# Two heads of an output pair worked together in two attentions, their value products alternating between the column halves of TensorE

## The chip, the cores and the metric

The kernel runs on one core of a Trainium2 chip. The metric is device time in microseconds (us). Three runs of the kernel before took 1254.60, 1258.07 and 1257.58 us; their median is 1257.58 us. The trace used below is one profiled execution, whose span from the first to the last instruction is 1254.4 us.

## The reference, cut to what matters

Two layers of a first block and then one layer of a second block are computed for 256 tokens of 1024 features. All of it is float32. Each layer multiplies the tokens by wide matrices, and beside that works several small attentions. Two of these are touched here.

The first block's sparse attention has 8 heads of 64 features in 2 groups. For 256 tokens its selected and its window part reduce to two causal attentions over the same 256 tokens, with different keys and values:

```
s_s = einsum('bgrqd,bgqnld->bgrqnl', qb, k_g);  p_s = masked_softmax(s_s, mask_s)
o_s = einsum('bgrqnl,bgqnld->bgrqd', p_s, v_g)
p_w = masked_softmax(einsum('bgrqd,bgkd->bgrqk', qb, kwb), mask_w)
o_w = einsum('bgrqk,bgkd->bgrqd', p_w, vwb)
return gb[..., 0:1] * o_c + gb[..., 1:2] * o_s + gb[..., 2:3] * o_w
```

The second block's block attention has 8 heads of 64 features. With 256 tokens there is one block, so it is one causal attention with a slope per head:

```
lo = where(dist_o >= 0, einsum('bhqd,bhkd->bhqk', qc, ko) * scale - slopes * dist_o, -inf)
out = einsum('bhqk,bhkd->bhqd', softmax(lo), vo)
```

Each head's result, transposed, has 64 rows. Two heads lie above each other in one tile of 128 rows: an output pair.

## The kernel before

**Main work.** The wide products split each float32 operand into a high and a low part (`hi`, `lo`; `hh`, `hl` for the activations) and multiply three times on TensorE. A unit of weights is 128 x 1024: it is loaded by a DMA to `raw`, copied by ScalarE to `hi` (line 435) and subtracted by VectorE to `lo` (line 439). Each sixth high part is made by GpSimd instead (line 433). While the convolution of the second block runs on VectorE, each fourth low part is made by GpSimd instead (line 437). There are four buffers for `hi` and four for `lo`.

**Order.** TensorE's instructions stand in the order in which Python emits them; a scheduler orders the other engines. The small attentions are generators. `mm` and `tr` add an estimated TensorE time to a clock; `yield 5100.0` in a generator means "go on when that clock is 5.1 us further", and `pump`, called inside the wide products, lets the generators that are due emit their next step. So a `yield` between two steps stands for the time the other engines have for what lies between them. TensorE itself never changes the order: a matmul that waits stops all behind it.

**PSUM.** Score and transpose tiles (`psm`) share three banks in turn; the results of attentions (`pso`) have one.

**Sparse attention of the first block** (`nsa_att`, run once in each of two layers). Head `2*pr + j` belongs to output pair `pr` (0 to 3) and lies in the rows `64*j` to `64*j + 63`. `scores0(pp, j)` works the first 128 queries of the heads of two pairs with one `j`, `scores1(pr, j)` the last 128 queries of one head; each with both branches (`w`), maximum (lines 895, 916), exponential (899, 920), sum, gate and scaling (905, 925). `transp(pr, j)` transposes one head's probabilities of both branches and copies them to `pts` (938 on ScalarE, 940 on VectorE). `pv(pr, j)` multiplies them with the values; output rows are the half `j`, so all four products of a call use one half of TensorE's columns. The scores of a head are emitted one head ahead of its transposes.

**Block attention of the second block** (`moba`). `scores(pp, j)` multiplies 64 rows (half `j`) of queries and keys and adds slope times distance by a bfloat16 product of all 128 rows (`SLP`, `DM`); the two kinds alternate. Two heads of one `j` are worked, then transposed and multiplied with the values one after the other, in one half of the columns each.

**Other places that have the same form.** In `nsa_cmp` (line 782) four products with 32 output rows each, at four column positions, are emitted in turn. In `gla` (the tiles `pas`) products of 64 rows alternate between the two row halves.

**The convolution** (`conv`) of the second block is 31 taps for each of four tiles on VectorE (lines 1432, 1435), emitted two taps per 1.5 us of the clock. `moba` runs beside it.

Of the kernel before, what the change touches and what calls it, by code (L numbers as in the profile page):

```python
# [98 lines left out]
def block_kernel(ctx, tc, x_in, mem_in, positions, ln_mix, w_in, b_merge, nsa_q_norm, nsa_k_norm,  # L99
# [778 lines left out]
    def nsa_att(VV, GT, T, c_mem, oh, ol):  # L878
# [7 lines left out]
        def scores0(pp, j):  # L886
            p0 = PS()
            for a in range(2):
                o0 = p0[:, 256 * a:256 * a + 256].rearrange("p (w k) -> p w k", w=2)
                q = QS[:, 4 * pp + 2 * a + j, 0:P]  # L890
# [12 lines left out]
            dve.tensor_tensor(r02, r02, gt4[:, 0, 4 * pp + j:4 * pp + j + 3:2, 1:3], op=OP.mult)  # L903
            for c in range(4):
                dve.tensor_scalar(e0[:, c], e0[:, c], r0[:, c:c + 1], None, op0=OP.mult)
            E0[pp, j] = e0
# [21 lines left out]
        def transp(pr, j):  # L928
            e0, e1 = E0[pr // 2, j], E1.pop((pr, j))
            res = []  # L930
            for w in range(2):
                pt = PS()
                tr(pt[:, 0:P], e0[:, 2 * (pr % 2) + w], IDF)
                for kt in range(2):
                    tr(pt[:, P + kt * P:2 * P + kt * P], e1[:, w, kt * P:kt * P + P], IDF)
                pts = T2("pts")[:, 0:384]
                if w == 0:
# [16 lines left out]
        order = [(2 * pp + a, j) for pp in range(2) for j in range(2) for a in range(2)]  # L954
        scores0(0, 0)
        yield 500.0
        scores1(*order[0])
# [421 lines left out]
    def layer_2(hT):  # L1379
# [105 lines left out]
        def moba():  # L1485
            UE = {}

            def scores(pp, j):
                rr = slice(64 * j, 64 * j + 64)
                p0, p1 = PS(), PS()  # L1490
                for a in range(2):
                    pr = 2 * pp + a
                    sl = SLP[:, 2 * pr + j, :]
                    mm(p0[:, a * P:a * P + P], CQ[rr, pr, 0:P], CK_[rr, pr, 0:P], True, False)
                    mm(p0[:, a * P:a * P + P], sl, DM[:, 0:P], False, True)
                    mm(p1[:, a * 256:a * 256 + 256], CQ[rr, pr, P:256], CK_[rr, pr, :], True, False)
                    mm(p1[:, a * 256:a * 256 + 256], sl, DM[:, P:384], False, True)
                n = SM([P, 4], "n0")
                dve.tensor_reduce(n[:, 0:2], v2(p0[:, 0:256]), op=OP.max, axis=AX, negate=True)
                dve.tensor_reduce(n[:, 2:4], v2(p1), op=OP.max, axis=AX, negate=True)  # L1500
                e0 = T2("pexp", (2, 128))
                e1 = T2("pexp", (2, 256))
                s = SM([P, 4], "s0")
                for a in range(2):
                    act(e0[:, a], p0[:, a * P:a * P + P], AF.Exp, bias=n[:, a:a + 1], accum_out=s[:, a:a + 1])
                    act(e1[:, a], p1[:, a * 256:a * 256 + 256], AF.Exp, bias=n[:, 2 + a:3 + a],
                        accum_out=s[:, 2 + a:3 + a])
                r = SM([P, 4], "r0")
                dve.reciprocal(r, s)
                for a in range(2):  # L1510
                    dve.tensor_scalar(e0[:, a], e0[:, a], r[:, a:a + 1], None, op0=OP.mult)
                    dve.tensor_scalar(e1[:, a], e1[:, a], r[:, 2 + a:3 + a], None, op0=OP.mult)
                UE[pp, j] = (e0, e1)

            for pp in range(2):
                yield from take_po()
                po = PO()
                for j in range(2):
                    rr = slice(64 * j, 64 * j + 64)
                    scores(pp, j)  # L1520
                    yield 9950.0
                    e0, e1 = UE.pop((pp, j))
                    for a in range(2):
                        h = 2 * (2 * pp + a) + j
                        pt = PS()
                        tr(pt[:, 0:P], e0[:, a], IDF)
                        for kt in range(2):
# [150 lines left out]
```

## Time and profile before

| what | value |
|---|---|
| runs (us) | 1254.60, 1257.58, 1258.07; median 1257.58 |
| span of the profiled execution | 1254.4 us |
| TensorE busy | 1234.7 us, 98% |
| VectorE busy | 846.5 us, 67% |
| ScalarE busy | 596.6 us, 48% |
| GpSimd busy | 244.6 us, 19% |
| weight loads of TensorE | 1108.0 us, 88% |
| HBM | 167 GB/s over the span |

The profile gives no time for the profiled execution beside its span; the span lies 0.2 us under the fastest of the three runs. "Busy" of TensorE counts a matmul from its start to the modelled end of its results, and matmuls overlap, so what a matmul costs TensorE is read from the distance between two starts, not from its duration. A float32 product appears as two records. Rows of one line, operation and tile that follow each other are merged, with their count (x8).

### The profile page before, as it was taken

The numbers are of one execution on the slowest core, as the hardware profiler recorded it, in microseconds if no ns is written. First come the engines' busy times: TensorE is split into PE (matmuls) and PEld (weight loads), VectorE is DVE, ScalarE is ACT, GpSimd is POOL, SyncE is SP. The second block draws the span as 40 slices with busy tenths as digits, with TensorE's granted clock in tenths as the row PEclk, the third lists the DMA queues.
The fourth block names the chain that finished last, engine by engine and source line by source line (L and its number), as shares of the span: only waits on it lengthen the run. The fifth ranks groups of instructions, "written<-read, shape, count | busy, mean of one in ns | idle before, by whom it ended". The sixth has DMA issues, their size and how long they took to land.

```text
span 1254.4 us, 21138 instructions
## 1 busy us (share of the span) xinstructions
PE 1234.7 (98%) x8317; PEld 1108.0 (88%) x8317; DVE 846.5 (67%) x1356; ACT 596.6 (48%) x956; POOL 244.6 (19%) x246
## 2 busy tenths in 40 slices
PE   8999999999999999999999999999999999999997
PEld 6897799998899899888799998989998988899996
DVE  5867878566754545567978566654545899956756
ACT  6567544444644444556644434544434343453532
POOL 2300320122112112200320023121211122111213
PEclk9999999999999999999999999999999999999999
DMA  8557533466566666656623566565665654445562
GB/s 269 177 157 203 155 101 102 137 185 199 185 185 185 189 183 196 184 153 173 191 68 112 155 167 190 177 193 179 198 187 171 202 155 137 153 135 169 179 219 74
DMA packets 165559, 211.00 MB, mean 168 GB/s; under 512 B 12065, under 2 KB 132277, under 8 KB 165460
## 3 DMA queue, kind: packets, MB, share of 16 engines
q1 hardware_dynamic: 165172, 209.49, 55.9%
q8 instruction: 65, 1.06, 0.3%
q0 software_dynamic: 288, 0.16, 0.1%
q14 instruction: 34, 0.28, 0.1%
HBM read 208.74 MB, written 1.05 MB: 167 GB/s over the span
## 4 chain that ended last, share of the span: by engine, by line
PE 84%; DVE 8%; POOL 2%; ACT 2%; issue 2%; DMA 0%; SPq 0%; POOLq 0%; ACTq 0%; DVEq 0%
PE acc L188 59%; PE psm L188 18%; PE psm L192 3%; PE pso L188 3%; DVE lo L439 3%; DVE b8x L1435 2%; POOL M L1150 2%; ACT hi L435 1%; PE acc L782 1%; ACT b8x L527 1%; DVE gate L1149 0%; DVE b8x L528 0%; DVE QB L1046 0%; ACT pexp L920 0%; DMA gtmp<-in_mem_norm 0%
## 5 line engine op out<-in xcount | busy, mean ns | idle before, releaser
L439 DVE TENSOR_TENSOR lo<-raw,hi 128x1024 fp32r<-128x1024 f32 (+1 forms) x359 | 451.5, 1261 | 264.0 <-ACT hi L435 203.5
L435 ACT ACTIVATE hi<-raw 128x1024 fp32r<-128x1024 f32 (+1 forms) x314 | 330.0, 1057 | 415.4 <-PE acc L188 254.7
L188 PE MATMUL acc<-hh,hi 128*128 128x256 f32 x960 | 278.7, 290 | 0.4 <-ACT hi L435 0.4
L188 PE MATMUL acc<-hh,lo 128*128 128x256 f32 x960 | 272.0, 283 | 1.7 <-DVE lo L439 1.6
L188 PE MATMUL acc<-hl,hi 128*128 128x256 f32 x960 | 271.9, 283 | 0.0
L188 PEld LDWEIGHTS acc<-hh,hi 128*128 128x128 f32 x960 | 184.0, 192 | 4.1 <-issue 2.5
L188 PEld LDWEIGHTS acc<-hh,lo 128*128 128x128 f32 x960 | 184.0, 192 | 2.3 <-DVE lo L439 2.3
L188 PEld LDWEIGHTS acc<-hl,hi 128*128 128x128 f32 x960 | 184.1, 192 | 1.1 <-DVE hl L528 0.2
L433 POOL TENSOR_SCALAR hi<-raw 128x1024 fp32r<-128x1024 f32 x55 | 67.0, 1219 | 477.8 <-PE acc L188 319.7
L188 PE MATMUL psm<-hh,hi 128*128 128x256 f32 x448 | 126.8, 283 | 0.0
L188 PE MATMUL psm<-hh,lo 128*128 128x256 f32 x448 | 126.8, 283 | 0.0
L188 PE MATMUL psm<-hl,hi 128*128 128x256 f32 x448 | 126.8, 283 | 0.0
L188 PE MATMUL acc<-hi,b8x 128*128 128x512 f32 (+1 forms) x336 | 104.0, 384 | 0.1
L188 PE MATMUL acc<-hi,oh 128*128 128x512 f32 x256 | 100.2, 391 | 0.0
L188 PE MATMUL acc<-lo,oh 128*128 128x512 f32 x256 | 99.8, 390 | 0.0
L188 PE MATMUL acc<-hi,ol 128*128 128x512 f32 x256 | 99.6, 389 | 0.0
L188 PE MATMUL acc<-hi,hh 128*128 128x512 f32 (+1 forms) x224 | 90.0, 402 | 0.0
L188 PE MATMUL acc<-lo,hh 128*128 128x512 f32 (+1 forms) x224 | 84.8, 378 | 2.2 <-DVE lo L439 2.2
L188 PEld LDWEIGHTS psm<-hl,hi 128*128 128x128 f32 x448 | 86.0, 192 | 0.5
L188 PEld LDWEIGHTS psm<-hh,hi 128*128 128x128 f32 x448 | 86.0, 192 | 0.5
L188 PEld LDWEIGHTS psm<-hh,lo 128*128 128x128 f32 x448 | 86.0, 192 | 0.0
L188 PE MATMUL acc<-hi,hl 128*128 128x512 f32 (+1 forms) x224 | 84.8, 378 | 0.0
(369 smaller groups left out, 2151.5 us busy)
## 6 DMA issues: line engine op xcount, KB each, us to landing
raw<-in_w_in SPq DMA_DIRECT2D x160, 512.0 KB
raw<-in_w_up SPq DMA_DIRECT2D x64, 512.0 KB
raw<-in_w_down SPq DMA_DIRECT2D x64, 512.0 KB
raw<-in_w_branch SPq DMA_DIRECT2D x28, 512.0 KB
raw<-in_w_out SPq DMA_DIRECT2D x24, 512.0 KB
raw<-in_cmp_w SPq DMA_DIRECT2D x32, 256.0 KB
raw<-in_mem_w_kv SPq DMA_DIRECT2D x15, 512.0 KB
raw<-in_w_branch SPq DMA_DIRECT2D x16, 256.0 KB
```

The costliest lines, as they stand in the source:

```text
L188: nc.tensor.matmul(o, l, r, start=start, stop=stop, skip_group_check=True)
L192: nc.tensor.transpose(o, i, ident)
L433: pool.tensor_scalar(hi, raw, 1.0, 1.0, op0=OP.mult, op1=OP.mult)
L435: act(hi, raw, AF.Copy)
L439: dve.tensor_tensor(lo, raw, f32(hi), op=OP.subtract)
L527: act(hi, src, AF.Copy, scale=scale)
L782: nc.tensor.matmul(ph[32 * j:32 * j + 32, k * 256:k * 256 + 256], R[k][:, lp].rearrange("p a b -> p (a b)"), rv[:, j, :], start=q == 0, st ...
L1150: pool.tensor_tensor(fl(M), fl(M), fl(g), op=OP.add)
L1435: dve.scalar_tensor_tensor(CV[:, cb], GLU[:, cb, t:t + 256], CWT[:, cb, t:t + 1], CV[:, cb], op0=OP.mult, op1=OP.add)
```

## The change

In both attentions the unit of work becomes the output pair, with both its heads. The products with the values then go head 0, head 1, head 0, head 1, so that consecutive products use the lower and the upper half of TensorE's columns in turn.

- `nsa_att`: `scores0(pr)` takes the first 128 queries of both heads of one pair; `transp(pr, w)` and `pv(pr, w)` take one branch of both heads. Per pair the steps are: scores1 of both heads, 5.1 us, transposes of branch 0, 2.0 us, products of branch 0, transposes of branch 1, scores0 of the next pair, 2.0 us, products of branch 1. The number of products, transposes and softmax steps stays.
- `moba`: `scores(pr)` emits the four 64-row products of a pair in turn, row half 0 and 1, in two banks, and then the four bfloat16 products. Maximum, reciprocal and scaling are done head by head, so there are 16 maxima where there were 8, and 8 reciprocals where there were 4. The scores of a pair are emitted before the transposes of the pair before it. The products with the values go by pair.

The core of the diff:

```diff
-        def pv(pr, j, po, pts2):
-            rr = slice(64 * j, 64 * j + 64)
-            vs = slice(64 * j, 64 * j + 64)
+        def pv(pr, w, po, t):
             a = pr % 2
-            o = po[rr, 256 * a:256 * a + 256]
-            for w, pts in enumerate(pts2):
-                mm(o, VVv[:, 0, w, vs], pts[:, 0:256], a == 0 and w == 0, False)
-                mm(o[:, 128:256], VVv[:, 1, w, vs], pts[:, 256:384], False, False)
+            for kt in range(2):
+                for j in range(2):
+                    js = slice(64 * j, 64 * j + 64)
+                    o = po[js, 256 * a + P * kt:256 * a + 256]
+                    mm(o, VVv[:, kt, w, js], t[j][:, 256 * kt:256 + P * kt], a == 0 and w == 0 and kt == 0, False)
...
-        for n, (pr, j) in enumerate(order):
+        for pr in range(4):
             pp = pr // 2
-            if n + 1 < 8:
+            for j in range(2):
                 yield 850.0
-                if n % 2 == 1:
-                    scores0(order[n + 1][0] // 2, order[n + 1][1])
-                scores1(*order[n + 1])
+                scores1(pr, j)
             yield 5100.0
-            t = transp(pr, j)
-            yield 3350.0
-            if n % 4 == 0:
+            t = transp(pr, 0)
+            yield 2000.0
+            if pr % 2 == 0:
                 yield from take_po()
                 po = PO()
-            pv(pr, j, po, t)
-            if n % 4 == 3:
+            pv(pr, 0, po, t)
+            t = transp(pr, 1)
+            if pr + 1 < 4:
+                scores0(pr + 1)
+            yield 2000.0
+            pv(pr, 1, po, t)
...
+            def scores(pr):
+                p = [PS(), PS()]
+                for q0, k1 in ((0, P), (P, 256)):
+                    for j in range(2):
+                        rr = slice(64 * j, 64 * j + 64)
+                        mm(p[j][:, q0:q0 + k1], CQ[rr, pr, q0:q0 + P], CK_[rr, pr, 0:k1], q0 == 0, False)
                 for j in range(2):
...
+                    mm(p[j][:, 0:P], sl, DM[:, 0:P], False, True)
+                    mm(p[j][:, P:384], sl, DM[:, P:384], False, True)
...
+                if pr + 1 < 4:
+                    yield 3000.0
+                    scores(pr + 1)
+                yield 6500.0
+                t = [transp(e) for e in UE.pop(pr)]
+                yield 2000.0
...
+                for kt in range(2):
+                    for j in range(2):
+                        h = 2 * pr + j
+                        o = po[64 * j:64 * j + 64, 256 * a + P * kt:256 * a + 256]
+                        mm(o, CVv[kt][:, h * 64:h * 64 + 64], t[j][:, 256 * kt:256 + P * kt], kt == 0, kt == 1)
```

**TensorE, products with the values of the sparse attention, first layer.** Here pts_285 and pts_287 are the two transposed tiles of a `transp`. Before, they are the two branches of one head:

```order
L188 MATMUL pso_293_1556<-pts_285_1501,n2_92_550 64x256
L188 MATMUL pso_293_1556<-pts_285_1501,n2_92_550 64x128
L188 MATMUL pso_293_1556<-pts_287_1507,n2_92_550 64x256
L188 MATMUL pso_293_1556<-pts_287_1507,n2_92_550 64x128
```

Now they are the two heads of a pair in one branch:

```order
L188 MATMUL pso_290_1538<-pts_285_1501,n2_92_550 64x256
L188 MATMUL pso_290_1538<-pts_287_1507,n2_92_550 64x256
L188 MATMUL pso_290_1538<-pts_285_1501,n2_92_550 64x128
L188 MATMUL pso_290_1538<-pts_287_1507,n2_92_550 64x128
```

A call still has four products; the 256-wide and the 128-wide one of the two halves now follow each other.

**TensorE, scores of the block attention.** The products of two g4 tiles have 64 rows, those of SLP and DM are bfloat16 and have 128. Before, for the two heads of one row half:

```order
L188 MATMUL psm_1845_10861<-g4_1783_10452,g4_1782_10451 128x128
L188 LDWEIGHTS SLP_10813
L188 MATMUL psm_1845_10861<-DM_10822,SLP_10813 128x128
L188 MATMUL psm_1846_10862<-g4_1783_10452,g4_1782_10451 128x256
L188 LDWEIGHTS SLP_10813
L188 MATMUL psm_1846_10862<-DM_10822,SLP_10813 128x256
L188 MATMUL psm_1845_10861<-g4_1783_10452,g4_1782_10451 128x128
L188 LDWEIGHTS SLP_10813
```

Now, for the two heads of the second pair:

```order
L188 MATMUL psm_1854_10911<-g4_1783_10452,g4_1782_10451 128x128
L188 MATMUL psm_1855_10912<-g4_1783_10452,g4_1782_10451 128x128
L188 MATMUL psm_1854_10911<-g4_1783_10452,g4_1782_10451 128x256
L188 MATMUL psm_1855_10912<-g4_1783_10452,g4_1782_10451 128x256
L188 LDWEIGHTS SLP_10813
L188 MATMUL psm_1854_10911<-DM_10822,SLP_10813 128x128
L188 LDWEIGHTS SLP_10813
L188 MATMUL psm_1854_10911<-DM_10822,SLP_10813 128x256
L188 LDWEIGHTS SLP_10813
L188 MATMUL psm_1855_10912<-DM_10822,SLP_10813 128x128
```

The four 64-row products stand together, in two banks (psm_1854 and psm_1855), and the bfloat16 products behind them.

**VectorE, beside the block attention.** The lo tiles are low parts of weights, the b8x rows are taps of the convolution. Before, two low parts and the next:

```order
L439 TENSOR_TENSOR lo_1864_10965<-raw_1862_10963,hi_1863_10964 128x1024
L1435 SCALAR_TENSOR_TENSOR b8x_1781_10450<-b8x_1750_10198,cw2_1739_10159,b8x_1781_10450 128x256 x3
L439 TENSOR_TENSOR lo_1867_10971<-raw_1865_10969,hi_1866_10970 128x1024
L1435 SCALAR_TENSOR_TENSOR b8x_1781_10450<-b8x_1750_10198,cw2_1739_10159,b8x_1781_10450 128x256 x4
L439 TENSOR_TENSOR lo_1883_11079<-raw_1881_11077,hi_1882_11078 128x1024
```

Now, from the same low part (its number is lo_1876) on:

```order
L439 TENSOR_TENSOR lo_1876_11002<-raw_1874_11000,hi_1875_11001 128x1024
L1433 SCALAR_TENSOR_TENSOR b8x_1781_10450<-b8x_1750_10198,cw2_1739_10159,b8x_1781_10450 128x256
L1499 TENSOR_REDUCE n0_1856_10921<-psm_1854_10911 128x1
L1500 TENSOR_REDUCE n0_1856_10921<-psm_1854_10911 128x1
L1499 TENSOR_REDUCE n0_1860_10932<-psm_1855_10912 128x1
L1500 TENSOR_REDUCE n0_1860_10932<-psm_1855_10912 128x1
L1433 SCALAR_TENSOR_TENSOR b8x_1781_10450<-b8x_1750_10198,cw2_1739_10159,b8x_1781_10450 128x256 x2
L439 TENSOR_TENSOR lo_1879_11008<-raw_1877_11006,hi_1878_11007 128x1024
L1507 RECIPROCAL r0_1859_10928<-s0_1858_10925 128x2
L1433 SCALAR_TENSOR_TENSOR b8x_1781_10450<-b8x_1750_10198,cw2_1739_10159,b8x_1781_10450 128x256
L1509 TENSOR_SCALAR pexp_1857_10924<-pexp_1857_10924,r0_1859_10928 128x128
L1509 TENSOR_SCALAR pexp_1857_10924<-pexp_1857_10924,r0_1859_10928 128x256
```

The softmax of the second pair now stands here, among these low parts; before, the second softmax stands behind the low part that follows these three.

## Rows read from the trace of the kernel before

**Rows 1.** The page: busy time of each engine with its share of the span and number of instructions, and the chain of work that ended last, by engine.

```profile
PE 1234.7 (98%) x8317; PEld 1108.0 (88%) x8317; DVE 846.5 (67%) x1356; ACT 596.6 (48%) x956; POOL 244.6 (19%) x246
...
PE 84%; DVE 8%; POOL 2%; ACT 2%; issue 2%; DMA 0%; SPq 0%; POOLq 0%; ACTq 0%; DVEq 0%
```

**Rows 2.** The timeline of TensorE's matmuls around four-column-position products (line 782) and one call of `pv` in the sparse attention of the first layer. Columns: start in us, length in us up to the last end, engine, line, operation, tiles, form, count.

```profile
133.03 0.39 PE L188 MATMUL acc<-lo,hh 128*128 128x512 f32 x1
133.26 0.40 PE L188 MATMUL acc<-hi,hl 128*128 128x512 f32 x1
133.58 0.64 PE L782 MATMUL acc<-raw,n 128*32 128x256 f32 x8
134.15 0.71 PE L188 MATMUL psm<-QB,b8x 128*128 128x128 f32 x4
...
135.49 1.51 PE L188 MATMUL pso<-pts,n 128*64 128x256 f32 x8
136.94 0.66 PE L192 MATMUL psm<-CF,n 128*128 128x128 f32 x4
```

**Rows 3.** Timeline of TensorE around the products that alternate between the row halves in the gated linear attention (tile `pas`), four products of 128 columns.

```profile
190.37 0.28 PE L188 MATMUL acc<-hl,hi 128*128 128x256 f32 x1
190.49 0.28 PE L188 MATMUL acc<-hh,lo 128*128 128x256 f32 x1
190.70 0.71 PE L188 MATMUL psm<-b8x,a 64*128 64x128 f32 x8
191.35 0.39 PE L188 MATMUL acc<-hh,hi 128*128 128x256 f32 x1
```

**Rows 4.** Timeline of TensorE in the block attention: the two products with the values of one head, and behind them the scores of two heads.

```profile
1053.92 0.86 PE L188 MATMUL pso<-pts,n 128*64 128x256 f32 x4
1054.71 0.48 PE L188 MATMUL psm<-g,g 64*128 64x128 f32 x2
1055.13 0.23 PE L188 MATMUL psm<-DM,SLP 128*128 128x128 bf16 x1
1055.29 0.70 PE L188 MATMUL psm<-g,g 64*128 64x256 f32 x2
1055.92 0.28 PE L188 MATMUL psm<-DM,SLP 128*128 128x256 bf16 x1
1056.13 0.48 PE L188 MATMUL psm<-g,g 64*128 64x128 f32 x2
...
1057.33 0.28 PE L188 MATMUL psm<-DM,SLP 128*128 128x256 bf16 x1
1057.37 0.36 PE L188 MATMUL acc<-hh,hi 128*128 128x256 f32 x1
```

**Rows 5.** All products with the values of both attentions, from the groups of TensorE by form. Columns: names and form, count of records, busy us and mean ns.

```profile
L188 PE MATMUL pso<-pts,n 128*64 128x256 f32 x80 | 25.0, 394 | 0.0
...
L188 PE MATMUL pso<-pts,n 128*64 128x128 f32 x80 | 15.3, 273 | 0.0
```

**Rows 6.** Busy time by stretch. Columns: stretch and its length, busy us (and count) of PE, PEld, DVE, ACT, POOL, then granted clock, DMA share, GB/s. The first two hold the sparse attention of the two layers; the others the block attention, in four parts.

```profile
118.00:245.00 127.00, 125.57 (x915) 111.10 (x915) 96.30 (x215) 64.67 (x147) 21.11 (x30) 0.99 0.45 131
600.00:722.00 122.00, 121.52 (x898) 107.26 (x897) 94.42 (x214) 62.56 (x145) 19.55 (x29) 1.00 0.46 136
...
1034.00:1050.00 16.00, 15.65 (x76) 12.02 (x75) 16.00 (x31) 7.08 (x15) 3.90 (x2) 1.00 0.47 144
1050.00:1068.00 18.00, 16.74 (x119) 14.25 (x119) 17.52 (x33) 6.08 (x14) 4.05 (x5) 1.00 0.42 130
1068.00:1090.00 22.00, 21.53 (x162) 19.45 (x163) 21.89 (x38) 10.75 (x21) 6.03 (x2) 1.00 0.45 138
1090.00:1116.00 26.00, 26.00 (x197) 23.09 (x195) 14.12 (x21) 11.45 (x21) 4.75 (x2) 1.00 0.54 167
```

**Rows 7.** TensorE's waits, by who was waited for (total us, times, longest), in the stretch 117 to 245 us (the first two rows) and in the stretch 1000 to 1136 us (the third).

```profile
PE psm L188 <- ACT ck L823: 1.1, 1, 1.1
PE psm L188 <- DVE a L1059: 0.4, 1, 0.4
...
PE acc L188 <- DVE lo L439: 3.8, 3, 2.2
```

**Rows 8.** Timeline of VectorE beside the block attention, and the row of TensorE that follows.

```profile
1061.88 1.22 DVE L439 TENSOR_TENSOR lo<-raw,hi 128x1024 fp32r<-128x1024 f32 x1
1063.01 0.42 DVE L1499 TENSOR_REDUCE n<-psm 128x2 f32<-128x256 f32 x1
1063.35 0.68 DVE L1500 TENSOR_REDUCE n<-psm 128x2 f32<-128x512 f32 x1
...
1065.22 0.18 DVE L1509 RECIPROCAL r<-s 128x4 f32<-128x4 f32 x1
...
1065.68 0.28 DVE L1511 TENSOR_SCALAR pexp<-pexp,r 128x128 f32<-128x128 f32 x1
...
1067.20 1.22 DVE L439 TENSOR_TENSOR lo<-raw,hi 128x1024 fp32r<-128x1024 f32 x1
...
1068.47 0.39 PE L188 MATMUL acc<-hh,lo 128*128 128x256 f32 x1 [1.30 <-DVE lo L439]
```

**Rows 9.** One softmax of the sparse attention of the first layer: the last product of its scores (CBT), its maximum and its last scaling on VectorE, and the transposes that read it.

```profile
202.61 0.28 PE L188 MATMUL psm<-CBT 128*128 128x256 bf16 x1
...
204.48 0.68 DVE L916 TENSOR_REDUCE n<-psm 128x2 f32<-128x512 f32 x1
...
211.22 0.61 DVE L925 TENSOR_SCALAR pexp<-pexp,r 128x256 f32<-128x256 f32 x2
...
222.99 0.60 PE L192 MATMUL psm<-CF,pexp 128*128 128x128 f32 x4
```

**Rows 10.** Weight loads of the products with the values, and of the products at four column positions (duration min, median, max in ns).

```profile
L188 PEld LDWEIGHTS pso<-pts,n x160: 132/137/137, 135.5 to 1115.8; 128*64 128x64 f32 x160
...
L782 PEld LDWEIGHTS acc<-raw,n x128: 106/108/109, 94.1 to 614.2; 128*32 128x32 f32 x128
```

**Rows 11.** A stretch in which the granted clock of TensorE was low (columns as in rows 6).

```profile
160.00:163.00 3.00, 3.00 (x14) 2.81 (x14) 2.36 (x8) 1.34 (x3) 1.10 (x3) 0.50 0.42 138
```

More of the change, by code (lines that the diff above doesn't have):

```diff
@@ L884, in nsa_att, with scores0 @@
         E0, E1 = {}, {}
-        def scores0(pp, j):
+        def scores0(pr):
             p0 = PS()
-            for a in range(2):
-                o0 = p0[:, 256 * a:256 * a + 256].rearrange("p (w k) -> p w k", w=2)
-                q = QS[:, 4 * pp + 2 * a + j, 0:P]
+            for j in range(2):
+                o0 = p0[:, 256 * j:256 * j + 256].rearrange("p (w k) -> p w k", w=2)
+                q = QS[:, 2 * pr + j, 0:P]
                 mm(o0, q, KH[:, :, j, 0:P], True, False)
@@ L1486, in moba @@
             UE = {}
[L1488 to L1492, printed above, removed]
-                    sl = SLP[:, 2 * pr + j, :]
[L1494 to L1513, printed above, removed]
@@ L1515, in moba @@
-            for pp in range(2):
-                yield from take_po()
-                po = PO()
-                for j in range(2):
[L1519 to L1527, printed above, removed]
-                            tr(pt[:, P + kt * P:2 * P + kt * P], e1[:, a, kt * P:kt * P + P], IDF)
-                        pts = T2("pts")[:, 0:384]
-                        act(pts, pt[:, 0:384], AF.Copy)
-                        yield 1050.0
-                        o = po[rr, a * 256:a * 256 + 256]
-                        mm(o, CVv[0][:, h * 64:h * 64 + 64], pts[:, 0:256], True, False)
-                        mm(o[:, 128:256], CVv[1][:, h * 64:h * 64 + 64], pts[:, 256:384], False, True)
-                act(AT[:, 2 * pp:2 * pp + 2], v2(po), AF.Copy)
-                free_po()
+            def scores(pr):
+                p = [PS(), PS()]
+                for q0, k1 in ((0, P), (P, 256)):
+                    for j in range(2):
+                        rr = slice(64 * j, 64 * j + 64)
+                        mm(p[j][:, q0:q0 + k1], CQ[rr, pr, q0:q0 + P], CK_[rr, pr, 0:k1], q0 == 0, False)
+                for j in range(2):
+                    sl = SLP[:, 2 * pr + j, :]
+                    mm(p[j][:, 0:P], sl, DM[:, 0:P], False, True)
+                    mm(p[j][:, P:384], sl, DM[:, P:384], False, True)
+                res = []
+                for j in range(2):
+                    n = SM([P, 2], "n0")
+                    dve.tensor_reduce(n[:, 0:1], p[j][:, 0:P], op=OP.max, axis=AX, negate=True)
+                    dve.tensor_reduce(n[:, 1:2], p[j][:, P:384], op=OP.max, axis=AX, negate=True)
+                    e = T2("pexp")[:, 0:384]
+                    s = SM([P, 2], "s0")
+                    cuts = (slice(0, P), slice(P, 384))
+                    for i, cs in enumerate(cuts):
+                        act(e[:, cs], p[j][:, cs], AF.Exp, bias=n[:, i:i + 1], accum_out=s[:, i:i + 1])
+                    r = SM([P, 2], "r0")
+                    dve.reciprocal(r, s)
+                    for i, cs in enumerate(cuts):
+                        dve.tensor_scalar(e[:, cs], e[:, cs], r[:, i:i + 1], None, op0=OP.mult)
+                    res.append(e)
+                UE[pr] = res
@@ new lines, in transp @@
+            def transp(e):
+                pt = PS()
+                for i in range(3):
+                    tr(pt[:, i * P:i * P + P], e[:, i * P:i * P + P], IDF)
+                pts = T2("pts")[:, 0:384]
+                act(pts, pt[:, 0:384], AF.Copy)
+                return pts
+            scores(0)
+            po = None
+            for pr in range(4):
+                a = pr % 2
+                if pr + 1 < 4:
[4 more added lines that the diff above has]
+                yield 2000.0
+                if a == 0:
+                    yield from take_po()
+                    po = PO()
+                for kt in range(2):
+                    for j in range(2):
+                        h = 2 * pr + j
+                        o = po[64 * j:64 * j + 64, 256 * a + P * kt:256 * a + 256]
+                        mm(o, CVv[kt][:, h * 64:h * 64 + 64], t[j][:, 256 * kt:256 + P * kt], kt == 0, kt == 1)
+                if a == 1:
+                    act(AT[:, pr - 1:pr + 1], v2(po), AF.Copy)
+                    free_po()
```

20 lines of the change are left out of this document (8 added, 12 removed).

## The prediction

> **What bounds the kernel now.** I read the page first. TensorE is busy for 98% of the span, no other engine for more than 67%, and 84% of the chain that ended last is TensorE's [rows 1]. So time is won where TensorE's own work gets shorter, and won for good only where the engines that feed it have room. The timeline of TensorE comes next, read by distances between starts: one call of `pv` (a 256-wide and a 128-wide product for each of two branches, eight records) holds TensorE from 135.49 to 136.94 us, 1.45 us [rows 2]; half as many in the block attention hold it 0.79 us [rows 4]. The difference, 0.66 us, is one 256-wide and one 128-wide product, by their columns 0.44 and 0.22 us. What is left of 0.79, 0.13 us, is paid once per call: the first start and the drain behind the last.
>
> Do two products in different parts of the array run side by side? The trace has both cases. Four 256-wide products at four column positions hold TensorE from 133.58 to 134.15, 0.57 us = 0.44 + 0.13: four cost what one costs [rows 2]. Four 128-wide products that alternate between row halves take 190.70 to 191.35, 0.65 us: two times 0.22 and 0.21 once [rows 3].
>
> Then the tables by stretch and the waits. In the sparse attention VectorE is busy for 96.3 of 127 us and 94.4 of 122 [rows 6], and in the first of them TensorE waits 1.5 us, for a free score bank and for a tile of VectorE's, never for a low part of weights [rows 7]. In the block attention the convolution runs on VectorE: it is busy 16.0 of 16, 17.5 of 18 and 21.9 of 22 us, then 14.1 of 26 [rows 6], and TensorE waits 3.8 us for low parts around it [rows 7], 1.3 of them at 1068.47, which starts 0.05 us after the low part of 1067.20 ends [rows 8].
>
> **The change, part by part.**
>
> Sparse attention, products with the values. A call still has four products, now in two pairs on different halves: 0.44 + 0.22 + 0.13 = 0.79 instead of 1.45 us. There are 8 calls in each of two layers: 16 x 0.66 = 10.5 us. The counts agree: 80 records of 256 columns are 40 products, 32 here and 8 in the block attention [rows 5]. Transposes, copies and softmax keep their number; they only move.
>
> Block attention, products with the values: 8 x 0.79 = 6.3 us become 4 x 0.79 = 3.2, a saving of 3.2 us.
>
> Block attention, scores: 1054.71 to 1057.37, 2.66 us for two heads [rows 4], four times. Now the 64-row products run as a 128-wide and a 256-wide pair: 0.22 + 0.44 + 0.21 = 0.87 us. Behind them come four bfloat16 products in a row, which the trace does not show. Lower bound: the last one before a full-width product lets the next start after 0.04 us, 0.16 in all; upper bound: 0.16 and 0.21, each twice, where a change to 64 rows follows, 0.74 in all [rows 4]. I take 0.12 each, the nearest row being a 256-wide product in an undisturbed run (190.37 to 190.49) [rows 3], 0.48. So 1.35 instead of 2.66, four times: 5.2 us saved (4.2 to 6.5).
>
> TensorE's work thus shrinks by 10.5 + 3.2 + 5.2 = 18.9 us. What of it reaches the end?
>
> In the sparse attention nothing else is full, so I keep the 10.5 and subtract what the new order can cost. Two transposes of a pair's second branch and the first scores of the next pair now follow each other and take all three score banks; the next user of a bank waits for ScalarE's copy, and behind it everything on TensorE. Before, such a wait was 1.1 us once [rows 7]. I take 0.5 us per layer, 1.0 in all; the bounds are 0 and six times 1.1, 6.6 us. The waits of before at this place may go too, up to 1.5 us. Kept: 9.5 us.
>
> In the block attention the 8.4 us (3.2 + 5.2) fall about evenly on the four stretches, 2.1 us each. In the first two VectorE has no free time and TensorE already waits for it: a shorter TensorE waits longer there, nothing kept. In the third VectorE is as full, but TensorE does not lag: half, 1.0. In the fourth VectorE has 12 us free: 2.1. VectorE's own work grows: per pair of heads two maxima of 0.42 and 0.68 become two 256-wide ones of 0.42 and two 128-wide ones (between 0.18, a reciprocal, and 0.42; I take the 0.28 of a 128-wide scaling), and one more reciprocal of 0.18 [rows 8]: 0.48 us, four times 1.9. About half of it meets full stretches. Kept: 1.0 + 2.1 - 0.9 = 2.2 us, between 0 and 8.4. The new order on VectorE also puts the second softmax ahead of low parts for which TensorE waits, and the second pair's scores need a fourth bank where there are three, so that TensorE stands until the first softmax is through. Both cost TensorE time only while VectorE is behind, so I count them within the nothing kept of the first two stretches.
>
> DMA queues, GpSimd's order of units and the number of copies do not change; with TensorE 1% faster the loads have room.
>
> Sum: 9.5 + 2.2 = 11.7 us. The profiled execution would take 1254.4 - 11.7 = 1242.7 us. Its span lies 3.2 us under the median of the runs, 1257.58; against that median the forecast is 1245.9 us. One disturbance is in both: behind sixteen 16-column products of the first layer the granted clock was 0.50 (1.2 GHz) in 160 to 163 us [rows 11], in the second layer not; at half pace three such microseconds cost about 1.5, so a run can move by that either way.
>
> **What the Trainium skill says against it.** The row first: eight weight loads of about 0.107 us and eight records of four products pass in 0.57 us [rows 2, 10], so neither the loads nor the first and second records of different products queue behind one another. The page "TensorE: Matmul & The Clock Gate", section "Part 3: Packing small matmuls", says that matmuls start and end strictly in order, and that a weight load overlaps running matmuls only where its row group differs; two column halves share all row groups. By strict order the sum would be about 5 us instead of 11.7; with exposed loads the kernel would become slower. This trace speaks against both, but for quarters of the columns, not for halves.
>
> **The rivals.**
>
> 1. VectorE gives way. Its order is made anew, and if low parts come earlier than the convolution needs them, the block attention keeps all of 8.4: 18.9 - 1.0, about 18 us, 1239.7. For: in the third stretch TensorE was 21.5 of 22 busy although VectorE was full [rows 6]. Against: 3.8 us of waits there already [rows 7]. 13%.
>
> 2. Halves overlap only in part. If the second record of head 0 must start before the first of head 1, two products take three slots in place of four: a call saves 0.33 us, 16 x 0.33 = 5.3, less 1.0 for waits, plus about 1 from the block attention: 1252.3. This is what strict order would do (the page above). Against: rows 2 and 3. 8%.
>
> 3. No effect. The halves do not overlap, or waits in the new order take 10 us back, at the banks or because copies that had 3.35 us of clock have 2.0. The time stays between 1254 and 1261. For: a wait on TensorE stops all behind it. Against: the copies are 0.5 us each with ScalarE and VectorE half and three quarters busy [rows 6]. 11%.
>
> 4. Slower, by the softmax. The scores of a head stood one head ahead of its transposes; now the last scores of a pair are followed by its transposes after 5.1 us of clock, about 5.5 us of TensorE's work. A softmax in the first layer had its scores at 202.61, its last scaling ended at 211.83, 9.2 us later, and its transposes came only at 222.99 [rows 9]. If it takes 9.2 again, TensorE stands 3.7 us before the transposes of pairs 1 to 3 in both layers, 22 us: 1245.9 + 22, about 1268. It outweighs the gain from 2 us each, that is from a softmax of 7.5 us. Against: in that case another softmax and a norm were queued ahead of it, and the first half's softmax now runs a step earlier. With exposed weight loads, eight of 0.137 us per call [rows 10], a call would take 0.79 + 1.1 = 1.9 instead of 1.45 us, 7 us slower over 16 calls; that I hold for less likely still. 6% together.
>
> **How the numbers follow.** The forecast has 62%. A change of 0.3%, 3.8 us, is about what a measurement of this kernel can tell from none. Faster by more: forecast, rival 1 and most of rival 2, 82%. Within: rival 3 and the rest of 2, 12%. Slower: 6%. The range goes from rival 1 less the clock's 1.5 us, 1238.5, to rival 2 with a little more waiting, 1253.
>
> **What would show it right or wrong.** In the profile after: `pso<-pts` in the sparse attention with eight records in about 0.8 us, not 1.1 or 1.45; the scores of a pair in about 1.3 us; TensorE's waits for low parts between 1000 and 1100 us longer by several us than before, up to 6; waits before the transposes (line 192, `pexp`) under 1 us each; the first 720 us shorter by 9 to 10 us. The forecast is wrong if eight records still take over 1 us, if TensorE waits for VectorE's scaling before most transposes, or if the stretch up to the end of the convolution is shorter by as much as TensorE's work in it.

## The result and the profile after

The changed kernel took 1245.59 us (median of 4 runs, 1243.95 to 1246.98), beside 1256.99 us for the kernel before (4 runs). The ratio is 0.9914, with a 95% interval of 0.9899 to 0.9929. A second measurement, on another chip and beside other runs of the kernel before, gave 1249.17 us (6 runs, 1245.70 to 1251.41) against 1255.88: 0.9948, interval 0.9933 to 0.9963. The two intervals do not overlap, so the gain is told here as 0.5 to 0.9%, 6.7 and 11.4 us. The longer times of the second measurement go with a lower mean granted clock of TensorE: 0.990 in its three longest runs, but 0.994 or 0.995 in its two shortest and in all four runs of the first. The forecast was 1245.9.

The page of the first execution, the row that answers to [rows 1]:

```profile
span 1242.2 us, 21154 instructions
...
PE 1216.0 (98%) x8317; PEld 1096.3 (88%) x8317; DVE 847.6 (68%) x1368; ACT 597.7 (48%) x957; POOL 239.8 (19%) x245
```

The number of matmuls is the same and TensorE's busy time is 18.7 us shorter, yet the span only 12.2.

TensorE's timeline, at one call of `pv` (answers to [rows 2]) and at the scores of one pair in the block attention (answers to [rows 4]):

```profile
132.48 0.87 PE L188 MATMUL pso<-pts,n 128*64 128x256 f32 x8
133.28 0.44 PE L192 MATMUL psm<-CF,pexp 128*128 128x128 f32 x2
...
1027.12 0.93 PE L188 MATMUL psm<-g,g 64*128 64x128 f32 x8
1027.98 0.51 PE L188 MATMUL psm<-DM,SLP 128*128 128x128 bf16 x4
1028.24 0.48 PE L188 MATMUL acc<-hi,hh 128*128 128x512 f32 x1
```

Eight records hold TensorE 0.80 us instead of 1.45, and all 20 calls do. The scores of a pair take 1.12 us instead of 2.66.

The groups by form answer to [rows 5]: as many records, 20.8 us together instead of 40.3, while one record lasts about as long as before (404 and 273 ns; 394 and 273 before). The mean says nothing of the gain; the sum falls because time in which two records lie beside each other is counted once.

```profile
L188 PE MATMUL pso<-pts,n 128*64 128x256 f32 x80 | 13.0, 404 | 0.0
L188 PE MATMUL pso<-pts,n 128*64 128x128 f32 x80 | 7.8, 273 | 0.0
```

Where along the program did the time come from? Both traces have the same 2344 products that read a low part, in the same order, so the same product can be found in both and its starts compared:

| up to product no. | before | after | after, second profile | gained in the stretch: first, second profile |
|---|---|---|---|---|
| 120, ahead of the sparse attention, layer 1 | 96.87 | 95.75 | 96.51 | 1.12, 0.36 |
| 340, behind it | 250.23 | 243.65 | 244.70 | 5.46, 5.17 |
| 1000, ahead of layer 2's | 593.57 | 586.96 | 587.99 | 0.03, 0.05 |
| 1200, behind it | 726.87 | 717.61 | 719.38 | 2.65, 1.91 |
| 1840, ahead of the block attention | 1014.12 | 1004.86 | 1006.62 | 0.00, 0.01 |
| 2060, behind it | 1132.26 | 1120.07 | 1122.88 | 2.93, 1.88 |

Three stretches gain, and nothing between them does. The first line is not the change's: nothing differs there, and over all kernels below this start lies between 0.4 us later and 1.4 us earlier than in the kernel before.

TensorE's waits in the three stretches, first layer, second layer and block attention, in that order (answer to [rows 7]):

```profile
PE psm L192 <- DVE a L1057: 0.8, 1, 0.8
PE psm L192 <- DVE n L867: 0.6, 1, 0.6
PE psm L188 <- DVE tmp L794: 0.5, 1, 0.5
PE psm L188 <- DVE a L1057: 0.4, 2, 0.2
...
PE psm L188 <- DVE tmp L794: 0.9, 1, 0.9
PE psm L188 <- ACT ck L823: 0.7, 1, 0.7
PE psm L192 <- DVE n L867: 0.6, 1, 0.6
PE psm L188 <- DVE a L1057: 0.4, 2, 0.2
...
PE acc L188 <- DVE lo L439: 3.2, 2, 2.2
PE psm L188 <- ACT pexp L1505: 3.1, 1, 3.1
PE acc L188 <- POOL lo L437: 0.6, 1, 0.6
PE acc L188 <- ACT hi L435: 0.4, 1, 0.4
```

The sums are 2.3, 2.6 and 7.3 us. All in the sparse attention are waits for a score bank (`psm`); in the second layer the kernel before had 0.4 us. In the block attention the waits for low parts are 3.8 us as before, and a wait of 3.1 us for a bank is new.

### The profile page after: what moved, and what is told of

Same layout as the page of the kernel before. It is cut to its first block, busy times and chain, and to the rows that moved or that the text cites. A ratio compares the mean times of both kernels' runs of the same rounds, so it can differ in the third digit from the quotient of the medians.

```text
span 1242.2 us, 21154 instructions
## 1 busy us (share of the span) xinstructions
PE 1216.0 (98%) x8317; PEld 1096.3 (88%) x8317; DVE 847.6 (68%) x1368; ACT 597.7 (48%) x957; POOL 239.8 (19%) x245
```

## Experiments

For each kernel below, the gain by stretch comes from the table's products, against the one profile of the kernel before.

**1. The two attentions apart.** One kernel has only `nsa_att` changed, one only `moba`.

```diff
 only the sparse attention:
-        def scores0(pp, j):
+        def scores0(pr):
...
 only the block attention:
-            def scores(pp, j):
+            def scores(pr):
...
```

> Only the sparse attention is changed; the block attention is that of the kernel before. The two traces show the changed kernel's TensorE 5.5 us ahead over the first layer's sparse attention and 2.7 us over the second's, 8.1 in all, and another 1.1 us from the start of the program, where nothing was changed. Theory A (the parts add up; the 1.1 us at the start is chance): 8 us faster than before, ratio about 0.9935, and the block attention as in the kernel before, with 3.8 us of waits for low parts. Theory B (the sparse attention's gain is partly luck of the clock, since the kernel before had a stretch at half clock in the first layer): 6 us, ratio 0.995, and a half-clock stretch in the first layer again.

> Only the block attention is changed; the sparse attention is that of the kernel before. Theory A (what the trace of the changed kernel shows of that stretch carries over): 2.9 us faster, ratio 0.9977, with a wait of about 3 us of the second pair's scores for a score bank. Theory B (how far VectorE is behind depends on when the stretch is reached): the wait is another, and the gain lies between 0 and 5 us.

Measured: sparse alone 1248.18 us, ratio 0.9936 (0.9914 to 0.9957); block alone 1253.58, 0.9974 (0.9961 to 0.9986). The stretches repeat. The kernel with the sparse attention alone gains 5.3 and 1.9 us in the two layers and nothing in the block attention. The kernel with the block attention alone gains 2.9 there, with a bank wait of 3.3 us; in its second layer it loses 1.6, where a stretch at half clock falls that the one profile of the kernel before does not have. The parts add up, as theory A of both has it. Theory B of the first was half right: the half clock came, but in the second layer. Windows of one microsecond of that run (columns as in [rows 6]):

```profile
637.00:638.00 1.00, 1.00 (x6) 0.59 (x7) 0.00 (x0) 1.00 (x8) 0.00 (x0) 0.50 0.00 0
638.00:639.00 1.00, 1.00 (x9) 0.48 (x6) 0.79 (x5) 0.45 (x3) 0.00 (x0) 0.50 0.00 0
```

**2. Is the alternation needed?**

```diff
-            for kt in range(2):
-                for j in range(2):
+            for j in range(2):
+                for kt in range(2):
                     js = slice(64 * j, 64 * j + 64)
```

and the same in `moba`.

> As the changed kernel, but the value products of a pair are issued head by head (both products of head 0, then both of head 1) in place of alternating. Theory A (a product on free columns starts whatever is queued ahead of it): a call still holds TensorE for 0.80 us, and the time is that of the changed kernel. Theory B (products start in the order of issue, so head 1 waits until head 0's second product has started): three slots in place of two, about 1.1 to 1.2 us a call, 20 calls by 0.33 us = 6 to 7 us slower than the changed kernel. Theory C (only neighbours of alternating halves overlap): 1.45 us a call, 13 us slower than the changed kernel.

Measured: 1248.30 us, 0.9935 (0.9914 to 0.9956). The timeline of this kernel:

```profile
133.80 0.88 PE L188 MATMUL pso<-pts,n 128*64 128x256 f32 x8
134.61 0.66 PE L192 MATMUL psm<-CF,pexp 128*128 128x128 f32 x4
```

0.81 us a call: theory A. The records do not name the head, but the forms tell it: a second 256-wide record starts 13 ns behind the first, while the two records of one product start 0.27 us apart. So head 1's first product starts 13 ns behind head 0's first, though head 0's second stands ahead of it in the program. The page "TensorE: Matmul & The Clock Gate" of the Trainium skill, "Part 3: Packing small matmuls", says that matmuls start and end strictly in order; this trace does not agree where the columns differ. Nor does the sentence above that TensorE itself never changes the order hold for the starts of such products. What makes the halves run together is that the two heads' products stand next to each other, not that they alternate. The run's 2.7 us over the first measurement is not this edit's: its sparse stretches are those of the run with the sparse attention alone (5.3 and 1.8), its bank wait in the block attention is 4.7 us, and both are found again in the second profile of the unaltered changed kernel below.

**3. The block attention: bank or VectorE?** The second pair's scores (1031.85 us) wait 3.1 us for a bank that the first pair's exponentials free:

```profile
1031.85 0.48 PE L188 MATMUL psm<-g,g 64*128 64x128 f32 x2
1035.47 1.04 PE L188 MATMUL psm<-g,g 64*128 64x128 f32 x6 [3.14 <-ACT pexp L1505]
1036.45 0.82 PE L188 MATMUL psm<-DM,SLP 128*128 128x128 bf16 x4
...
1037.50 0.63 PE L188 MATMUL acc<-lo,hh 128*128 128x512 f32 x1
1037.93 0.63 PE L188 MATMUL acc<-hi,hl 128*128 128x512 f32 x1
```

Behind the wait a 512-wide product takes 0.43 us from start to start, later 0.23: the clock is at half, as the windows show:

```profile
1037.00:1038.00 1.00, 1.00 (x5) 0.81 (x4) 1.00 (x3) 0.17 (x1) 0.00 (x0) 0.50 0.00 0
1038.00:1039.00 1.00, 1.00 (x4) 0.81 (x3) 1.00 (x3) 0.36 (x1) 0.00 (x0) 0.50 0.00 0
```

Why the exponentials are late is seen on VectorE. The first pair's scores are done soon after 1028 us, but their maxima (lines 1499 and 1500) start only at 1033.86, behind nine taps of the convolution. The rows of VectorE, then one of GpSimd, then the first exponential on ScalarE:

```profile
1028.15 5.79 DVE L1433 SCALAR_TENSOR_TENSOR b8x<-b8x,cw,b8x 128x256 f32<-128x256 f32 x9
1033.86 0.28 DVE L1499 TENSOR_REDUCE n<-psm 128x1 f32<-128x128 f32 x1
...
1027.49 2.99 POOL L437 TENSOR_TENSOR lo<-raw,hi 128x1024 fp32r<-128x1024 f32 x1 [13.06 <-ACT hi L435]
...
1034.51 0.37 ACT L1505 ACTIVATE pexp<-psm,n 128x128 f32<-128x128 f32 x1 [7.09 <-DVE n L1500]
```

One of the nine taps took 2.62 us, the other eight 0.47 each; the long one ran beside GpSimd's subtraction of a low part. So about 2.1 of the 5.8 us go with that meeting, not with the number of taps.

First, the next pair's scores come later:

```diff
-                    yield 3000.0
+                    yield 6500.0
                     scores(pr + 1)
-                yield 6500.0
+                yield 3000.0
```

> As the changed kernel, but in the block attention the next pair's scores are issued about 4 us of TensorE's work later (yields 3000 and 6500 swapped), so that the first pair's softmax can have left its two score banks. Theory A (the 3.1 us wait for a bank, and the half clock behind it, some 2 to 3 us by the longer holds, are what the new order costs): the wait is under 0.5 us, and the kernel is 4 to 5.5 us faster than the changed one, ratio to before about 0.987. Theory B (VectorE is full until the convolution ends, so TensorE waits for it anyway): the wait goes, but waits for low parts between 1040 and 1090 us grow by as much, and the gain is under 1 us.

Measured: 1250.61 us, 0.9956 (0.9938 to 0.9975), the whole gain of the stretch gone (0.15 us worse than before), and another 1.3 us lost behind it, at a wait of 1.1 us for a low part. Both theories missed. The waits of 1000 to 1130 us:

```profile
PE psm L192 <- ACT pexp L1505: 7.4, 2, 4.1
PE acc L188 <- DVE lo L439: 2.2, 1, 2.2
PE psm L188 <- ACT pexp L1505: 1.4, 1, 1.4
```

The transposes now come so soon behind the scores that they want the bank which the late softmax still holds. The wait for low parts is only the 2.2 us ahead of the scores: TensorE stands elsewhere in the meantime. Next, the scores behind the value products, so that two banks do for them:

```diff
-                if pr + 1 < 4:
-                    yield 3000.0
-                    scores(pr + 1)
-                yield 6500.0
+                yield 9500.0
...
+                if pr + 1 < 4:
+                    scores(pr + 1)
```

> As the changed kernel, but in the block attention the next pair's scores are issued behind the value products of the pair before (no softmax overlaps the next pair's scores), so two score banks are enough for them. Theory A (three banks for four users are the price, 3.1 us of waiting at the second scores plus some 2 us at half clock): no wait for a bank over 0.5 us, low parts come as early as before, 4 to 5 us faster than the changed kernel over this stretch. Theory B (VectorE is full until the convolution ends, and its lateness shows wherever TensorE next needs it): the wait for a bank goes, waits for low parts or for the softmax before the transposes take its place, and the stretch gains under 1.5 us.

Measured: 1245.15 us, 0.9903 (0.9883 to 0.9923); the stretch gains 4.4 us in place of 2.9 and 1.9. No wait for a bank is left, and low parts are late instead:

```profile
PE acc L188 <- DVE lo L439: 6.0, 4, 2.2
```

The gain is 1.5 us more than in the first profile, the edge of theory B, and 2.5 more than in the second, beyond it; theory A had 4 to 5 and no later low parts. The bank was the form of the wait, but not its source. The direct test takes half the work of the convolution off VectorE, in both kernels; every second tap is left out, so they compute another convolution:

```diff
-                    dve.scalar_tensor_tensor(CV[:, cb], GLU[:, cb, t:t + 256], CWT[:, cb, t:t + 1], CV[:, cb],
-                                             op0=OP.mult, op1=OP.add)
+                    if t % 2 == 1:
+                        dve.scalar_tensor_tensor(CV[:, cb], GLU[:, cb, t:t + 256], CWT[:, cb, t:t + 1], CV[:, cb],
+                                                 op0=OP.mult, op1=OP.add)
```

> As the changed kernel, but every second tap of the convolution is left out (15 of 30 products per block, evenly spread), which takes some 25 us of work from VectorE in the block attention's stretch. To be compared with the kernel before with the same taps left out. Theory A (VectorE is what keeps TensorE's saved 8.4 us from arriving): no wait of over 0.5 us for a score bank at the second pair's scores, and the block attention's stretch is 8 us shorter than in the kernel before with half the taps. Theory B (three banks are too few whatever VectorE does): a wait of 2 us or more stays at the second scores, and the stretch is at most 6 us shorter.

> The kernel before with every second tap of the convolution left out, as the base for the run on the changed kernel with the same taps left out. If VectorE is what TensorE waits for there, the 3.8 us of waits for low parts between 1000 and 1136 us go, and the stretch is 4 to 6 us shorter than in the kernel before (the slow clock behind the longest of them goes too); if not, under 1 us.

Measured: 1236.27 us changed, 1252.53 before. The stretch is 3.3 us shorter in the kernel before with half the taps (a little less than expected: the wait of 2.2 us ahead of the scores stays, and the slow clock behind it that the expectation counted is not in the one profile of the kernel before), and 11.0 in the changed one: 7.7 us between the two, against 2.9 and 1.9 with the full convolution. The second scores stand where they stood, 4.72 us behind the first, with the same three banks, and wait for nothing:

```profile
1028.12 0.93 PE L188 MATMUL psm<-g,g 64*128 64x128 f32 x8
1028.97 0.51 PE L188 MATMUL psm<-DM,SLP 128*128 128x128 bf16 x4
1032.84 0.93 PE L188 MATMUL psm<-g,g 64*128 64x128 f32 x8
1033.70 0.50 PE L188 MATMUL psm<-DM,SLP 128*128 128x128 bf16 x4
```

Theory A: VectorE is what keeps the gain from arriving. Two things go with the left-out taps: their own time and the meetings with GpSimd, in this stretch 1 tap of over 2 us in place of 5. No run parts the two.

**4. The sparse attention: crowded banks or VectorE's queue?**

```diff
+            if pr + 1 < 4:
+                yield 850.0
+                scores0(pr + 1)
+                yield 4250.0
+            else:
+                yield 5100.0
...
             t = transp(pr, 1)
-            if pr + 1 < 4:
-                scores0(pr + 1)
```

> As the changed kernel, but in the sparse attention the first scores of the next pair are issued ahead of the pair's transposes, 850 of clock behind its last scores, instead of right behind the second transposes. The changed kernel waits 2.2 us in the first layer's sparse stretch and 2.3 in the second's, nearly all for score banks, against 1.5 and 0.4 in the kernel before. Theory A (transposes and scores back to back crowd the three banks): the waits fall to 1 us or less in each layer, 2 to 3 us faster than the changed kernel over both stretches. Theory B (TensorE has become shorter and the engines that empty the banks have not): the waits move to other places with about the same sum, and the stretches differ by under 0.7 us in all.

Measured: 1250.02 us, 0.9945 (0.9925 to 0.9966). The waits in the two layers are 2.6 and 2.7 us, at other places, so theory A is out. Theory B has the waits right but not the time: the first layer gains 3.9 us where the first profile has 5.5, both at full clock, and the second loses 1.6 where that has a gain of 2.7, with between 6 and 7 us at half clock behind the 16-column products. Why the first layer is longer was not traced. What VectorE was doing at one such wait, 0.9 us up to 616.52 in the second layer of the changed kernel, for a bank that the reduction of line 794 empties:

```profile
613.35 0.18 DVE L901 RECIPROCAL r<-s 128x4 f32<-128x4 f32 x1 [1.21 <-ACT pexp L899]
613.57 0.17 DVE L903 TENSOR_TENSOR r<-r,GT 128x4 f32<-128x4 f32 x1
613.76 1.23 DVE L439 TENSOR_TENSOR lo<-raw,hi 128x1024 fp32r<-128x1024 f32 x1
614.90 0.87 DVE L905 TENSOR_SCALAR pexp<-pexp,r 128x128 f32<-128x128 f32 x4
615.69 0.68 DVE L794 TENSOR_REDUCE tmp<-psm 128x128 f32<-128x512 f32 x1
```

VectorE stood idle 1.2 us for the new softmax's exponentials with the reduction queued behind, then did a low part and four scalings first. So work was taken off VectorE, in both attentions, on top of the kernel with the scores behind the values:

```diff
-                if j == 0:
-                    act(pts, pt[:, 0:384], AF.Copy)
-                else:
-                    dve.tensor_copy(pts, pt[:, 0:384])
+                act(pts, pt[:, 0:384], AF.Copy)
...
-                        dve.tensor_scalar(e[:, cs], e[:, cs], r[:, i:i + 1], None, op0=OP.mult)
+                        act(e[:, cs], e[:, cs], AF.Copy, scale=r[:, i:i + 1])
```

> Built on the run with the scores behind the values, with two pieces of VectorE's work given to ScalarE: in the sparse attention the second copy of each pair's transposes (0.55 us, 8 a layer), in the block attention the four scalings of each pair's softmax (1.1 us a pair). Theory A (waits come from VectorE's queue, where what empties a bank or makes a low part stands behind other work): the sparse stretches get 0.5 to 1 us shorter each and the block stretch 1 to 2.5 us shorter than in the run with the scores behind the values. Theory B (VectorE's queue waits for ScalarE's exponentials, and more work on ScalarE makes these later): no stretch gets shorter by over 0.3 us, or they get longer.

Measured: 1242.96 us, 0.9898 (0.9885 to 0.9911), on the same chip as the second measurement of the changed kernel (0.9948): faster than both kernels by intervals that lie apart. From the run it is built on (0.9903, 0.9883 to 0.9923) the time does not tell it apart, so what the two pieces are worth is read from the stretches alone. The first layer gains 6.1 us (5.1 in the run it is built on; 5.1 to 5.5 in the six profiles with this layer in the new order and at full clock). The second layer's waits are 1.4 us in place of 2.6:

```profile
PE psm L192 <- DVE ck L830: 0.6, 1, 0.6
PE psm L192 <- DVE a L1054: 0.6, 1, 0.6
PE psm L188 <- DVE a L1054: 0.2, 1, 0.2
```

but its gain, 1.5 (2.6 in the run it is built on), carries a half-clock stretch of between 6 and 7 us. The block stretch gains 5.0 in place of 4.4, less than theory A had: 2.0 us of waits for ScalarE's high parts are new there.

**5. The changed kernel again.**

> The changed kernel itself once more, for what differs between executions of one program. If the 1.1 us at the start and the clock behind the 16-column products are chance: the same stretches but for shifts of up to 1.5 us at the start and about 1.7 us per half-clock stretch of 3.3 us, in either layer, and the block attention the same to 0.2 us; median between 1244 and 1249. If they belong to the change: the start again 1 us early and no half clock in either layer.

Measured: the 1249.17 us given above, just over what was expected. The start was 0.4 us early instead of 1.1, the second layer had a half-clock stretch, and the block attention was not the same to 0.2 us: 1.9 in place of 2.9. There the second scores were

```profile
1032.02 0.49 PE L188 MATMUL psm<-g,g 64*128 64x128 f32 x2
1037.22 1.22 PE L188 MATMUL psm<-g,g 64*128 64x128 f32 x5 [4.71 <-ACT pexp L1505]
```

1.57 us more waiting than in the first profile. In the first profile the clock had fallen to half behind the wait for a low part at 1018.69, and TensorE lost 1.6 us there (in the second it stayed at full); what it lost it then waited less. The time at which the bank came free was not TensorE's to set. That is VectorE's bound once more, shown by an accident of the clock. The longer stand was followed by more than 6 us at half clock instead of some 3, which is about the 1.0 us between the profiles.

## Why the prediction was right, and where it was not

**The overlap** (0.79 us a call, 10.5 us in the sparse attention): right. The calls took 0.80; from first start to the next instruction's start they held TensorE 11.55 us per layer, now 6.41: 5.1 us a layer, 10.3 in all. The rival by strict order is out, by the call's time and more sharply by the heads in turn.

**The scores of the block attention** (1.35 us for a pair, 5.2 us saved): right in kind, mis-sized: 1.12 where nothing waits, 6.2 us. The four bfloat16 products cost 0.26 us together, near the lower bound of 0.16.

**Waits in the new order of the sparse attention** (1.0 us in all, bounds 0 and 6.6): this is the term that failed. In the second layer, where both profiles ran at full clock, 5.1 us saved became 2.7 gained: 2.5 us lost, 2.2 of them new waits in the table. In the first layer the profile's 5.5 contain the half-clock stretch of [rows 11], which the changed kernel did not have; one such stretch cost 1.6 us in the second layer of the run with the block attention alone. That puts the first layer's own gain near 3.9 and the loss there near 1.3. Lost in all about 3.8 in place of 1.0, kept about 6.5 in place of 9.5 (estimates, from these rows). A second way gives a little less: the changed kernel with half the convolution had a half-clock stretch in its first layer too, and gained 4.5 there, so the loss in that layer would be 0.6 and in all 3.1. The first 720 us, forecast to be shorter by 9 to 10, are shorter by 9.3 and 7.5 in the two profiles, 1.1 and 0.4 of that at the start. The place was named, the score banks. The step assumed that only ScalarE's copies empty them; most were emptied late by VectorE. At the wait looked at above, the new softmax stood ahead in its queue; for the others that is not shown.

**The block attention** (2.2 us kept of 8.4, VectorE full): right in the reason, which the half convolution shows, and in the sum, 2.9 and 1.9 in two profiles; not in the terms of the four stretches (0, 0, 1.0 and 2.1, less 0.9). Compare the product that starts at 1090.32 us in the kernel before, where its convolution ends. From the start of the stretch up to there the changed kernel has lost 1.4 us (2.5 in the second profile), some of it to the clock. The 4.4 us that it gains, in both profiles, all come behind. So the sum is near by terms that offset each other. The waits given as the reason for the first two stretches were misread, too. Of the 3.8 us for low parts [rows 7], the longest wait lies ahead of the block attention, whose first scores start at 1034.79, and the 1.3 us in the third stretch; in the first two TensorE waited only 0.3:

```profile
1027.95 0.50 PE L188 MATMUL acc<-lo,hh 128*128 128x512 f32 x1 [2.24 <-DVE lo L439]
...
1049.85 0.39 PE L188 MATMUL acc<-hh,lo 128*128 128x256 f32 x1 [0.30 <-DVE lo L439]
```

What was to show the reason was wrong in part, too: the waits for low parts did not grow, 3.8 us as before. VectorE's lateness appeared at the second pair's scores, the stall that the forecast named and counted within the nothing kept. That it would bring a stretch at half clock was not foreseen; when the scores moved away (4.4 us kept), the same lateness appeared as waits for low parts.

**The sum**: 11.7 forecast, 12.2 in the profile, 11.4 and 6.7 by the medians of the two measurements. The first is closer than the terms: 1.1 us at the start and 1.6 of clock are chance that helped. Without them the profile would give 9.5, and the second profile gave 9.4 us up to TensorE's last product, with chance of its own for and against. The range held both measurements. The near hit of the first measurement is in part luck.

**Rivals**: VectorE gave no way (1). No effect (3) is out by both intervals; waits did take some of the gain back, but 3 to 4 us in the sparse attention, not 10. Slower by the softmax (4) is out: no wait for a scaling of the sparse softmax stands among the waits of either layer. Exposed weight loads, the second half of (4), are out by the 0.80 us of a call.

## What to carry to other kernels

When TensorE gets shorter in a stretch where a second engine is full, look for that engine's lateness at every place where it lets something go (a bank, a low part, a probability), since moving one wait away brings up another; what freed the gain here was work taken off that engine: with half the convolution 7.7 us arrived in place of 2.9 and 1.9. Two products on different halves of the columns need only stand next to each other. And a change of under 1% is to be read by stretches between the same products in two traces, with the clock beside them: here two measurements of one kernel differ by 3.6 us.

## What the runs showed of the hardware

- Products on free columns overtake: eight records in issue order head by head took 0.81 us, alternating 0.80.
- The half clock behind the sixteen 16-column products came in the first layer in 1 and in the second in 4 of the 7 profiles with the sparse attention in the new order of steps (one of them with its heads in turn), for some 3 us each, and for 6 to 7 in other kernels; the same program has it in one execution and not in the next. Behind the 2.2 us wait for a low part near 1020 us the clock fell in the first profile of the changed kernel and not in the second.
- A tap of the convolution that ran beside GpSimd's subtraction of a low part could take five times as long. In the first profile of the changed kernel GpSimd made 10 low parts, 7 of them met taps, and each time one tap took 2.0 to 2.6 us; the 109 taps that met none took at most 0.49. The kernel before has 7 such taps as well. A low part given to GpSimd thus saved VectorE 1.2 us and, where it met a tap, was followed by about 2.1 us lost there (an estimate: 2.6 less 0.48); no run takes GpSimd's low parts away.
